# Attention weights split into fp16 hi and lo in the first stage, kept in DRAM, and loaded as fp16

## The chip, the cores and the metric

The kernel runs on one core of a Trainium2 chip. The metric is the device time of one execution in microseconds (us), and the median of several runs is what versions are compared by. The engines of the core, by the names of the profile: PE is TensorE (matmuls; PEld is its weight loads), DVE is VectorE, ACT is ScalarE, POOL is GpSimd, SP is SyncE, which only issues DMA transfers here. PEq, SPq and so on are the instruction queues of these engines.

## The reference

A decoder trunk of two layers on a sequence of 512 tokens, width 1024. Layer A is a gated short convolution, layer B is sparse attention over a key/value side that is computed once after layer A; each is followed by a squared-ReLU MLP. All inputs and the output are float32.

```python
# layer 0 (A)
h = rms_norm(x, norm_mix[0])
b, c, u = split(h @ a_w_in, 3)                  # 1024 -> 3 x 1024
x = x + (b * conv3(c * u)) @ a_w_out
x = x + square(relu(rms_norm(x, norm_mlp[0]) @ mlp_w1[0])) @ mlp_w2[0]   # 1024 -> 4096 -> 1024
# shared key/value side
kv = rms_norm(x, kv_norm) @ w_kv                # 6 parts of 4 groups x 64
k_cmp = silu(blocks(kv[0]) @ phi_k_w1) @ phi_k_w2     # 31 blocks, 2048 -> 256 -> 64
v_cmp = silu(blocks(kv[1]) @ phi_v_w1) @ phi_v_w2
# layer 1 (B)
q, gates = rms_norm(x, norm_mix[1]) @ b_w_qg    # 16 heads x 64, and 48 gates
o = gates[0]*attn(q, k_cmp, v_cmp) + gates[1]*attn(q, k_sel, v_sel) + gates[2]*attn(q, k_win, v_win)
x = x + o @ b_w_o
x = x + square(relu(rms_norm(x, norm_mlp[1]) @ mlp_w1[1])) @ mlp_w2[1]
out = rms_norm(x, final_norm)
```

The three attentions are causal, with a relative-position bias added to the logits. With these sizes every selected block and the whole window lie within the sequence, so that two of them are full causal attentions and one goes over 31 compressed blocks.

## The kernel before

**Products.** Every matmul is fp16, and keeps nearly fp32 precision by a split: a value is scaled and written as hi (fp16) and lo = value - hi (fp16), and a product is hi x hi + hi x lo + lo x hi (`mm3`, lines 338 to 341). Activations are kept transposed, features on the partitions, 512 tokens along the free axis; a weight tile of 128 x 128 is the stationary operand.

**Weights.** They come in pieces, listed in order of use in `pieces`. An ordinary piece is 1024 fp32 columns on 128 partitions (512 KB). It goes through three steps. `load_piece` loads it on SP's queue into a staging tile `wst` (three of them). `convert_piece` makes `whi` on ACT (line 193) and `wlo` on DVE (line 194), four buffers of each. `next_piece` hands it to the matmuls. Conversions run two pieces ahead of use (`ahead`), and a conversion is followed by as many loads as staging tiles are free. Within attention the conversion is made in two halves of 512 columns (`ahead_fine`, `convert_piece(512)`), emitted between matmuls. Weights of the second MLP matrices go another way (`down_blocks`, tiles `wst2`, lines 180 to 183), which combines blocks of them first.

**The first stage** (tile pool `first`, lines 222 to 482). The input is transposed chunk by chunk on PE (`x_chunk`: `x0h` on ACT, `x0l` on DVE, line 288 and 289), while six accumulators collect the first pass of the in-projection. The row scale (`x_rstd`, then `rs_r`, `rb`, `rb2`) is applied as the accumulators are read. Passes 1 to 3 have three products each (`pc`, `pu`, `pb`), each of two pieces and 48 matmuls, with six PSUM banks in rotation; the reader of `pc` is `cv_t` (line 446). Then come the four passes of the out projection, with the residual, its squares and the split for the MLP. The bias table goes through DRAM (`ext_d`). Then the first MLP follows (pool `hidden_a`).

**Attention** (pool `attn`). First keys, values, gates and the queries of group 0 are made one after the other. Then a list of items is worked off: a `Full` item is one head of one block of 128 queries in one of the two full branches, a `Cmp` item one block of a group in the compressed branch. An item has the steps st0 (logits on PE, bias and minimum on DVE as `at_s` and `at_m`, exponential on ACT as `at_p`), st1 (transpose on PE, `at_ph` on ACT), st2 (`at_pl` on DVE), st3 (product with the values) and st4 (transposition of the output for the projection). The steps of several items are interleaved by fixed leads:

```python
lead = {1: 2, 2: 3, 3: 4, 4: 6}
...
credit += 1.7 if i < 64 else 0.9
```

Between items the background generator advances by `credit` steps: raw keys, query group 1, phi of the keys, raw values, phi of the values, query groups 2 and 3, half of the output projection. `queries` writes `Q` on ACT and POOL; `raw` writes `kr_hl` and copies it by DMAs on SP into `big`, which the phi matmuls read. The other half of the output projection follows the last item, and then the second MLP (pool `hidden_b`).

Within each engine the instructions run in the order of its own queue. That order is set when the kernel is built, by a scheduler that takes program order as priority and may move an instruction ahead where its operands are due earlier.

Of the kernel before, what the change touches and what calls it, by code (L numbers as in the profile page):

```python
# [10 lines left out]
F32 = mybir.dt.float32  # L11
# [37 lines left out]
def body(ctx, tc, x, rel_bias, norm_mix, norm_mlp, mlp_w1, mlp_w2, a_w_in, a_conv_w, a_w_out,  # L49
         kv_norm, w_kv, cmp_pe_k, cmp_pe_v, phi_k_w1, phi_k_w2, phi_v_w1, phi_v_w2,  # L50
         b_w_qg, b_w_o, final_norm, ident_c, onehot_c, out):
    nc = tc.nc
# [23 lines left out]
    def cols(w, c0, n, scale, k0=0, kn=8):  # L76
        pieces.append((w[k0 * 128:(k0 + kn) * 128, c0:c0 + n].rearrange("(c p) n -> p c n", p=128),
                       (kn, n), scale))
# [13 lines left out]
    def mlp_pieces(layer):  # L92

        for half in range(2):
            for p in range(8 * half, 8 * half + 8):
                up_pair(mlp_w1[layer], p)
            for p in range(4):
                down_blocks(mlp_w2[layer], p, half)

    def block(w, c0, scale=SW, k0=0, kn=8):  # L100
        for k in range(k0, k0 + kn, 4):
            cols(w, c0, 256, scale, k, 4)
# [12 lines left out]
        block(w_kv, part * 256)  # L115
    cols(b_w_qg[0], 1024, 48, SW)
    block(b_w_qg[0], 0)
    block(w_kv, 0)
    block(b_w_qg[0], 256)
    block(phi_k_w1, 0, SW, 0, 16)  # L120
# [6 lines left out]
    for g in range(0, 4, 2):  # L127
        for p in range(4):
            cols(b_w_o[0], p * 256, 256, SW, 2 * g, 4)
    mlp_pieces(1)  # L130

    NS, NW, AHEAD, PIECE = 3, 4, 2, 1024
# [11 lines left out]
    def blocked(i):  # L144
        return pieces[i][1] is None

    def load_piece():
        i = pos["dma"]
        if i >= len(pieces):
            return  # L150
        src, shape, _ = pieces[i]
        if shape is None:
            t = wk[0].tile([128, PIECE2], F32, name="wst2", bufs=NS2)
            for k, u in enumerate(src):
                nc.sync.dma_start(t[:, k * PIECE:k * PIECE + 512].rearrange("p (j n) -> p j n", j=2), u)
        else:
            t = wpool.tile([128, PIECE], F32, name="wst", bufs=NS)
            a, n = shape
            v = t[:, :a * n].rearrange("p (a n) -> p a n", a=a)
            if len(src.shape) == 4:  # L160
                v = v.rearrange("p a (j n) -> p a j n", j=2)
                for j in range(2):
                    nc.sync.dma_start(v[:, :, j], src[:, :, j])
            else:
                nc.sync.dma_start(v, src)
        staged[i] = t
        pos["dma"] += 1

    def convert_piece(step=1024):

        i = pos["cv"]
        if i >= len(pieces):
            return
        _, shape, sc = pieces[i]
        t = staged.pop(i)
        pos["cv"] += 1
        if shape is None:
            b = t.rearrange("p (k b n) -> p k b n", k=2, n=128)
            for e, o, x, y in W_SUMS:
                DVE.tensor_tensor(b[:, :, o], b[:, :, x], b[:, :, y], op=e)  # L180
            hi, lo = (wk[0].tile([128, 2, 7, 128], F16, name=n, bufs=NW2) for n in ("whi2", "wlo2"))
            ACT.activation(hi, b[:, :, 1:], AF.Copy, scale=sc)  # L182
            DVE.scalar_tensor_tensor(lo, b[:, :, 1:], sc, hi, op0=OP.mult, op1=OP.subtract)  # L183
            ready[i] = (hi, lo)
            yield
        else:
            a, n = shape
            hi = wpool.tile([128, PIECE], F16, name="whi", bufs=NW)
            lo = wpool.tile([128, PIECE], F16, name="wlo", bufs=NW)
            for s in range(0, a * n, step):  # L190
                e = min(s + step, a * n)
                w = t[:, s:e]
                ACT.activation(hi[:, s:e], w, AF.Copy, scale=sc)  # L193
                DVE.scalar_tensor_tensor(lo[:, s:e], w, sc, hi[:, s:e], op0=OP.mult, op1=OP.subtract)  # L194
                yield
            r = lambda w: w[:, :a * n].rearrange("p (a n) -> p a n", a=a)
            ready[i] = (r(hi), r(lo))
        while pos["dma"] < len(pieces):
            like = [j for j in range(pos["cv"], pos["dma"]) if blocked(j) == blocked(pos["dma"])]
            if len(like) >= (NS2 if blocked(pos["dma"]) else NS):  # L200
                break
            load_piece()

    def next_piece():

# [11 lines left out]
    def drain(gen):  # L217
        for _ in gen:
            pass
# [169 lines left out]
    for p in range(4):  # L389
        pc, pu, pb = [], [], []  # L390
        if p == 0:
            for dst in (pc, pu, pb):
                dst += [acc(), acc()]

            def first_pairs(dst, w, c):
                part = 1 if dst is pc else 2 if dst is pu else 0
                for m in range(2):
                    mm3(dst[m], [u[:, part, m * 128:(m + 1) * 128] for u in w], [u[:, c] for u in xs],
                        c == 0, c == 7)

            hi = [x_chunk(0), x_chunk(1)]
            for c in range(6):
                w = next_piece()
                if c == 0:
                    load_x(6, 8)
                for dst in (pc, pu, pb):
                    first_pairs(dst, w, c)
                with tc.issue_after(hi[c + 1].ins):
                    drain(ahead())
                hi.append(x_chunk(c + 2))  # L410
            with tc.issue_after(hi[5].ins):
                r0 = x_rstd()
            pr = broadcast_rows(r0)
            rby = row_tile(pr, SY / (SW * SX))
            rb2 = ftile("rb2", 1)
            DVE.tensor_tensor(rb2, rby, rby, op=OP.mult)
            ws = [next_piece(), next_piece()]
        if p == 1:

            ext = wk[0].tile([H, EXT], F32, name="ext")  # L420
            POOL.memset(ext[:, 0:PAD], NEG)
            pe_ = bank("e")
            PE.matmul(pe_[0:H, :], relb, onehot, start=True, stop=True)
            ACT.activation(ext[:, PAD:], pe_[0:H, :], AF.Copy, scale=SL)
            ext_d = dram.tile([H, EXT], F32, name="ext_d")
            nc.scalar.dma_start(ext_d, ext)
            pet = const.tile([128, 2, 16], F32, name="pet")
            pp = bank("e")
            for i in range(2):
                PE.transpose(pp[:, i * 16:(i + 1) * 16], pe_in[:, i], ident[0:16, 0:16])  # L430
            ACT.activation(pet.rearrange("p a b -> p (a b)"), pp[:, 0:32], AF.Copy)
        for dst in (pc, pu, pb):
            if p:
                dst += [acc(), acc()]
                pair(xs, dst)
            else:
                for k in range(2):
                    first_pairs(dst, ws[k], 6 + k)
            drain(ahead())
            for m in range(2):  # L440
                ch = 2 * p + m
                if dst is pc:
                    if m == 0:
                        tmps = []
                    t = ftile("cv_t", 2)
                    DVE.scalar_tensor_tensor(t, pc[m], 1.0 / (SY * SY), rb2, op0=OP.mult, op1=OP.mult)
                    tmps.append(t)
                elif dst is pu:
                    if m == 0:
                        convs = []  # L450
                    v = ftile("cv_v", 2, S + 2)
                    DVE.memset(v[:, 0:2], 0.0)
                    DVE.tensor_tensor(v[:, 2:], pu[m], tmps[m], op=OP.mult)
                    cw = [vec[:, 40 + 8 * k + ch:41 + 8 * k + ch] for k in range(3)]
                    o = ftile("cv_o", 2)
                    ACT.activation(o, v[:, 0:S], AF.Copy, scale=cw[0])
                    for k in (1, 2):
                        DVE.scalar_tensor_tensor(o, v[:, k:k + S], cw[k], o, op0=OP.mult, op1=OP.add)
                    convs.append(o)
                else:  # L460
                    b = ftile("cv_b", 2)
                    DVE.tensor_tensor(b, pb[m], rby, op=OP.mult)
                    DVE.tensor_tensor(b, b, convs[m], op=OP.mult)
                    split_to(ys[0][:, ch], ys[1][:, ch], b)
# [6 lines left out]
    for p in range(4):  # L471
        po = [acc(), acc()]
        pair(ys, po)
        if p < 3:
            drain(ahead())
        for m in range(2):
            residual_in(po[m], 2 * p + m, 1.0 / (SY * SW))
            ss.add(X[:, 2 * p + m])
        for m in range(2):
            split_gain(xs, 2 * p + m, X[:, 2 * p + m], "mlp0")  # L480
        drain(ahead())
    first.__exit__(None, None, None)


# [754 lines left out]
```

## Time and profile before

| what | value |
|---|---|
| median of 3 runs | 1150.83 us (1150.39 to 1152.06) |
| the profiled execution | 1151.28 us, its span 1149.5 us |
| mean granted TensorE clock | 0.994 |
| DMA moved | 115.76 MB, mean 101 GB/s |

The span is from the first to the last instruction. Line numbers (L193) are those of the kernel before. "out<-in" are the tiles that an instruction writes and reads; a row of waits reads "who waited <- for whom: us in total, times, longest". Successive matmuls overlap in the records, so that a busy PE is not one at its peak.

### The profile page before, as it was taken

The numbers are of one execution on the slowest core, as the hardware profiler recorded it, in microseconds if no ns is written. First come the engines' busy times: TensorE is split into PE (matmuls) and PEld (weight loads), VectorE is DVE, ScalarE is ACT, GpSimd is POOL, SyncE is SP. The second block draws the span as 40 slices with busy tenths as digits, with TensorE's granted clock in tenths as the row PEclk, the third lists the DMA queues.
The fourth block names the chain that finished last, engine by engine and source line by source line (L and its number), as shares of the span: only waits on it lengthen the run. The fifth ranks groups of instructions, "written<-read, shape, count | busy, mean of one in ns | idle before, by whom it ended". The sixth has DMA issues, their size and how long they took to land.

```text
span 1149.5 us, 20386 instructions
## 1 busy us (share of the span) xinstructions
PE 1106.0 (96%) x7959; PEld 694.1 (60%) x7959; DVE 837.8 (73%) x1604; ACT 582.7 (51%) x983; POOL 162.2 (14%) x211
## 2 busy tenths in 40 slices
PE   9999999999999999999999899999999999999996
PEld 4444444447884458868466665765444688445885
DVE  4755557765897557988487898997985588754795
ACT  4523235345333444457679778676644534343452
POOL 0000000422000220000120023111132200022031
PEclk9999999999999999999999999999999999999998
DMA  6433235433433333314333530111643343330231
GB/s 208 130 92 110 92 111 174 119 93 93 127 98 108 109 110 107 97 55 122 110 79 99 143 94 19 57 38 38 186 126 99 88 126 110 104 99 19 75 92 74
DMA packets 149379, 115.76 MB, mean 101 GB/s; under 512 B 8612, under 2 KB 146564, under 8 KB 149284
## 3 DMA queue, kind: packets, MB, share of 16 engines
q1 hardware_dynamic: 146736, 109.47, 31.8%
q10 hardware_dynamic: 2260, 4.40, 1.3%
q8 instruction: 62, 1.02, 0.4%
q0 software_dynamic: 288, 0.61, 0.2%
q14 instruction: 33, 0.27, 0.1%
HBM read 110.22 MB, written 2.14 MB: 98 GB/s over the span
## 4 chain that ended last, share of the span: by engine, by line
PE 49%; DVE 20%; ACT 12%; issue 8%; POOL 6%; DMA 4%; SPq 0%; DVEq 0%; ACTq 0%; POOLq 0%
POOL ml_z L501 6%; PE a L340 4%; PE a L339 4%; PE a L341 4%; DVE wlo L183 4%; DMA wst<-mlp_w_dram 4%; ACT rh L502 3%; PE b L339 3%; PE b L340 3%; PE b L341 3%; PE c L341 3%; PE c L339 3%; PE c L340 3%; DVE wst L180 3%; DVE wlo L194 3%
## 5 line engine op out<-in xcount | busy, mean ns | idle before, releaser
L193 ACT ACTIVATE whi<-wst 128x1024 f16<-128x1024 f32 (+2 forms) x171 | 142.2, 857 | 128.3 <-PE b L340 40.0
L194 DVE SCALAR_TENSOR_TENSOR wlo<-wst,whi 128x1024 f16<-128x1024 f32 (+2 forms) x171 | 168.1, 990 | 47.3 <-ACT whi L193 47.1
L501 POOL TENSOR_TENSOR ml_z<-ml_z 128x256 f32<-128x256 f32 x128 | 101.1, 811 | 604.5 <-ACT ml_z L499 403.9
L182 ACT ACTIVATE whi<-wst 128x1792 f16<-128x1792 f32 x64 | 107.0, 1692 | 132.6 <-DVE wst L180 107.8
L341 PEld LDWEIGHTS <-wlo 128*128 128x128 f16 x1024 | 100.1, 98 | 109.3 <-DVE wlo L194 0.7
L339 PEld LDWEIGHTS <-whi 128*128 128x128 f16 x1024 | 100.4, 98 | 108.1 <-issue 3.7
L503 DVE TENSOR_TENSOR rl<-ml_z,rh 128x1792 f16<-128x1792 f32 x32 | 64.8, 2025 | 136.9 <-ACT rh L502 136.9
L340 PEld LDWEIGHTS <-whi 128*128 128x128 f16 x1024 | 100.2, 98 | 105.0 <-issue 1.7
L183 DVE SCALAR_TENSOR_TENSOR wlo<-wst,whi 128x1792 f16<-128x1792 f32 x64 | 129.8, 2033 | 3.6 <-ACT whi L182 3.6
L180 DVE TENSOR_TENSOR wst<-wst 128x256 f32<-128x256 f32 x256 | 105.9, 455 | 24.1 <-DMA wst<-mlp_w_dram 23.1
L502 ACT ACTIVATE rh<-ml_z 128x1792 f16<-128x1792 f32 x32 | 54.3, 1697 | 103.4 <-POOL ml_z L501 103.4
L550 PEld LDWEIGHTS <-wlo 128*128 128x128 f16 x896 | 88.1, 98 | 16.6 <-issue 5.1
L549 PEld LDWEIGHTS <-whi 128*128 128x128 f16 x896 | 88.1, 98 | 14.8 <-issue 3.9
L548 PEld LDWEIGHTS <-whi 128*128 128x128 f16 x896 | 88.2, 98 | 11.0
L499 ACT ACTIVATE ml_z<-ml_t 128x1024 f32<-128x1024 f32 x32 | 33.8, 1057 | 90.5 <-DVE ml_t L497 90.5
L341 PE MATMUL b<-xsh,wlo 128*128 128x512 f16 x208 | 78.8, 379 | 0.0
L340 PE MATMUL b<-xsl,whi 128*128 128x512 f16 x208 | 78.8, 379 | 0.0
L339 PE MATMUL b<-xsh,whi 128*128 128x512 f16 x208 | 78.7, 379 | 0.0
L922 ACT ACTIVATE at_p<-at_s,at_m 128x128 f32<-128x128 f32 (+3 forms) x128 | 71.3, 557 | 13.4 <-DVE at_m L919 13.0
L549 PE MATMUL a<-rl,whi 128*128 128x256 f16 x256 | 70.3, 275 | 4.6 <-DVE rl L503 4.6
L339 PE MATMUL c<-xsh,whi 128*128 128x512 f16 x192 | 72.8, 379 | 0.0
L340 PE MATMUL c<-xsl,whi 128*128 128x512 f16 x192 | 72.8, 379 | 0.0
(312 smaller groups left out, 2757.5 us busy)
## 6 DMA issues: line engine op xcount, KB each, us to landing
wst<-mlp_w_dram SPq DMA_DIRECT2D x256, 256.0 KB, 3.4
wst<-a_w_in_dram SPq DMA_DIRECT2D x18, 512.0 KB, 3.6
wst<-w_kv_dram SPq DMA_DIRECT2D x12, 512.0 KB, 3.7
T<-ext_d ACTq DMA_DIRECT2D x4, 1056.0 KB, 6.0
wst<-a_w_out_dram SPq DMA_DIRECT2D x8, 512.0 KB, 3.5
wst<-b_w_qg_dram SPq DMA_DIRECT2D x8, 512.0 KB, 4.3
wst<-b_w_o_dram SPq DMA_DIRECT2D x8, 512.0 KB, 3.5
wst<-a_w_in_dram SPq DMA_DIRECT2D x8, 384.0 KB, 5.5
```

The source lines that it names most:

```text
L180: DVE.tensor_tensor(b[:, :, o], b[:, :, x], b[:, :, y], op=e)
L182: ACT.activation(hi, b[:, :, 1:], AF.Copy, scale=sc)
L183: DVE.scalar_tensor_tensor(lo, b[:, :, 1:], sc, hi, op0=OP.mult, op1=OP.subtract)
L193: ACT.activation(hi[:, s:e], w, AF.Copy, scale=sc)
L194: DVE.scalar_tensor_tensor(lo[:, s:e], w, sc, hi[:, s:e], op0=OP.mult, op1=OP.subtract)
L339: PE.matmul(ps, w[0], xs[0], start=start, stop=False)
L340: PE.matmul(ps, w[0], xs[1], start=False, stop=False)
L341: PE.matmul(ps, w[1], xs[0], start=False, stop=stop)
L501: POOL.tensor_tensor(z[:, o], z[:, a], z[:, b], op=e)
L502: ACT.activation(rh[0][:, p], z[:, 1:8], AF.Copy)
L548: PE.matmul(acc7[i], wh, xh, start=c == 0 and not other, stop=False, skip_group_check=other)
L549: PE.matmul(acc7[i], wh, xl, start=False, stop=False, skip_group_check=other)
```

## The change

The 26 full pieces that are used from the raw keys on (`w_kv` parts 0 and 1, `b_w_qg` groups 1 to 3, the first weights of both phi, `b_w_o`) are listed in `early`. In the first stage `keep_load` loads them as fp32 on SP into `kp_w` (two tiles), and `keep` makes `kp_h` on ACT and `kp_l` on DVE (two tiles each) and stores both in DRAM on POOL's queue. `keep(2)` stands behind each of the nine products of passes 1 to 3 and in the four passes of the out projection. In attention such a piece is loaded as fp16 straight into `whi` and `wlo` by two DMAs on SP, as soon as it is less than three pieces ahead of the next use, and its conversion is only a hand-over. The other pieces go the old way.

```diff
@@ the list of pieces
     block(b_w_qg[0], 0)
+    early = [len(pieces)]
     block(w_kv, 0)
...
+    early = [i for i in range(early[0], len(pieces)) if pieces[i][1][0] * pieces[i][1][1] == 1024]
+    kept = {}
     mlp_pieces(1)
@@ load_piece
-        if shape is None:
+        if i in early:
+            t = []
+            for name, d in zip(("whi", "wlo"), kept[i]):
+                w = wpool.tile([128, PIECE], F16, name=name, bufs=NW)
+                nc.sync.dma_start(w, d)
+                t.append(w.rearrange("p (a n) -> p a n", a=shape[0]))
+        elif shape is None:
@@ convert_piece
-        if shape is None:
+        if i in early:
+            ready[i] = tuple(t)
+        elif shape is None:
...
+        load_pieces()
+
+    def load_pieces():
         while pos["dma"] < len(pieces):
-            like = [j for j in range(pos["cv"], pos["dma"]) if blocked(j) == blocked(pos["dma"])]
-            if len(like) >= (NS2 if blocked(pos["dma"]) else NS):
+            i = pos["dma"]
+            if i in early:
+                full = i >= pos["use"] + NW - 1
+            else:
+                like = [j for j in range(pos["cv"], i) if j not in early and blocked(j) == blocked(i)]
+                full = len(like) >= (NS2 if blocked(i) else NS)
+            if full:
                 break
             load_piece()
+
+    keeping = {}
+
+    def keep_load(n):
+        for i in early[len(keeping):len(keeping) + n]:
+            src, (a, m), _ = pieces[i]
+            keeping[i] = wk[0].tile([128, PIECE], F32, name="kp_w", bufs=2)
+            nc.sync.dma_start(keeping[i].rearrange("p (a n) -> p a n", a=a), src)
+
+    def keep(n):
+        for i in early[len(kept):len(kept) + n]:
+            t, sc = keeping[i], pieces[i][2]
+            hi, lo = (wk[0].tile([128, PIECE], F16, name=m, bufs=2) for m in ("kp_h", "kp_l"))
+            ACT.activation(hi, t, AF.Copy, scale=sc)
+            DVE.scalar_tensor_tensor(lo, t, sc, hi, op0=OP.mult, op1=OP.subtract)
+            kept[i] = [dram.tile([128, PIECE], F16, name=f"kept{i}{m}") for m in "hl"]
+            for d, w in zip(kept[i], (hi, lo)):
+                nc.gpsimd.dma_start(d, w)
+            keep_load(1)
@@ in passes of the in-projection, behind each product
             drain(ahead())
+            if p == 0 and dst is pb:
+                keep_load(2)
+            if p:
+                keep(2)
@@ in passes of the out projection
         drain(ahead())
+        keep(2)
+    assert len(kept) == len(early)
```

## The prediction

> **What bounds the kernel now.** I read the page first, for the busy times and their course over the span.
>
> ```profile
> span 1149.5 us, 20386 instructions
> PE 1106.0 (96%) x7959; PEld 694.1 (60%) x7959; DVE 837.8 (73%) x1604; ACT 582.7 (51%) x983; POOL 162.2 (14%) x211
> PE   9999999999999999999999899999999999999996
> DVE  4755557765897557988487898997985588754795
> ```
>
> The reader is to see that TensorE (PE) is in its highest digit almost everywhere, and that VectorE (DVE) is half idle in slices 3 to 6 and seven to nine tenths busy in slices 21 to 29. PE's busy time flatters it, since successive matmuls overlap in the records, so the next view was the busy time by stages: conv mixer (45 to 137 us), its out projection (137 to 179), attention (540 to 820), and within attention the conversions alone (DVE's line L194, then ScalarE's, ACT's, line L193).
>
> ```profile
> core 0: us, PE busy (x) PEld busy (x) DVE busy (x) ACT busy (x) POOL busy (x), PEclk, DMA share, GB/s
> 45.00:137.00 92.00, 92.00 (x426) 41.22 (x425) 52.60 (x71) 28.11 (x34) 0.00 (x0) 1.00 0.34 104
> 137.00:179.00 42.00, 42.00 (x196) 19.06 (x195) 24.45 (x31) 16.71 (x22) 0.00 (x0) 1.00 0.33 101
> 540.00:820.00 280.00, 260.93 (x2638) 170.83 (x2637) 231.31 (x717) 208.20 (x565) 45.13 (x59) 1.00 0.28 80
> ...
> sum 280.00, DVE 44.21; mean DVE 3.68
> ...
> sum 280.00, ACT 38.14; mean ACT 3.18
> ```
>
> In the first two rows PE never pauses, while DVE is busy 57% and ACT 30 to 40% of the time: work added there on DVE and ACT has room. In attention PE is idle for at least 280 - 260.9 = 19.1 us, DVE is busy 83% and ACT 74%, and the conversions are 44.2 of DVE's 231.3 us. The third view is who makes PE wait there, matmuls and weight loads (PEld) taken apart.
>
> ```profile
> PE c L928 <- DVE at_pl L934: 5.4, 7, 1.5
> PE b L914 <- DVE at_m L919: 3.2, 6, 1.5
> PE c L886 <- POOL o L963: 2.3, 2, 2.0
> PE b L914 <- POOL Q L739: 1.9, 3, 0.9
> PE d L946 <- ACT at_ph L931: 1.4, 5, 0.6
> ...
> PEld c L928 <- DVE at_pl L934: 9.9, 22, 1.6
> PEld L946 <- ACT at_ph L931: 5.9, 14, 0.8
> PEld L914 <- POOL Q L739: 3.9, 4, 1.4
> PEld c L886 <- POOL o L963: 3.4, 4, 2.5
> PEld c L928 <- ACT at_p L922: 2.2, 4, 1.5
> ```
>
> Many short waits, not one long one: the softmax chain of an item goes PE, DVE, ACT, PE, ACT, DVE, PE, and each engine takes its queue in order, so a conversion of 0.7 us that stands ahead of an `at_pl` or `at_ph` delays the next transpose or product. Those on DVE and ACT add up to 5.4 + 9.9 + 3.2 + 1.4 + 5.9 + 2.2 = 28.0 us, those on GpSimd (POOL) to 11.5 us. So attention is bound by PE's work plus some 19 to 40 us of hand-overs, and the first stage by PE alone.
>
> **Removed from attention.** 26 pieces of 1024 columns (w_kv and phi first weights, queries 1 to 3, the output projection) lose their split. They were split in halves:
>
> ```profile
> L194 DVE SCALAR_TENSOR_TENSOR wlo<-wst,whi 128x512 f16<-128x512 f32 x54 | 37.8, 713 | 7.3 <-ACT whi L193 7.3
> L193 ACT ACTIVATE whi<-wst 128x512 f16<-128x512 f32 x54 | 32.3, 624 | 14.5 <-PE a L340 6.0 <-issue 4.0 <-PE a L700 2.5
> ```
>
> 52 halves are 52 x 0.713 = 37.1 us of DVE and 52 x 0.624 = 32.4 us of ACT. None of it is PE's own work, so the most that can come back is the 28.0 us of waits on these two engines, and the least is nothing, if the waits are plain latency of the chain. Between these ends I go by how full the queues are. DVE's busy to idle time is 231.3 to 48.7, a ratio of 4.7; without the 37.1 us, in a stage 15 us shorter, it is 194.2 to 70.8, or 2.7, 42% less. ACT's goes from 2.9 (208.2 to 71.8) to 2.0, 32% less. Waits that shrank alike would give 28.0 x 0.42 = 12 us. I take **15 us**, because the conversions are among the longest instructions of the queue and come in runs of two to four, so they cause more than their share; this is an estimate. The waits on POOL stay.
>
> **Added in the first stage: the split.** The same 26 pieces are converted there at 1024 columns; near rows of this size and form are
>
> ```profile
> 33.64 1.05 ACT L193 ACTIVATE whi<-wst 128x1024 f16<-128x1024 f32 x1
> 34.72 1.22 DVE L194 SCALAR_TENSOR_TENSOR wlo<-wst,whi 128x1024 f16<-128x1024 f32 x1 [0.43 <-ACT whi L193]
> ...
> ACT whi L193 <- PE c L340: 28.8, 7, 4.1
> ```
>
> 26 x 1.22 = 31.7 us of DVE and 26 x 1.05 = 27.3 us of ACT, over about 150 us. From 45 to 179 us DVE would go from 77 to about 106 of 134 us and ACT from 45 to 67. The cover is PE's unbroken work and the lead of the conversions: ACT waits for PE to free a weight buffer (28.8 us in 7 waits on one line alone), so conversions run ahead of need, and a `kp` instruction ahead of one is absorbed. If that cover failed at the four pass ends, a yl or a residual two instructions late would cost about 2.4 us each; I put **1 us** (0 to 5).
>
> **The start is where there is no cover.** In the order of the built instructions the first six splits stand before about 45 us: four `kp_h` ahead of the last x0h on ACT, two more ahead of `rb`, and two `kp_l` on DVE between the steps of the first rstd. The chain there before the change:
>
> ```profile
> 26.57 0.69 ACT L288 ACTIVATE x0h<-e,vec 128x512 f16<-128x512 f32 x1 [2.90 <-PE e L372]
> 36.00 0.30 ACT L296 ACTIVATE rs_r<-ss,eps 128x4 f32<-128x4 f32 x1
> 37.15 0.67 ACT L288 ACTIVATE x0h<-e,vec 128x512 f16<-128x512 f32 x1
> 39.86 0.16 DVE L303 SCALAR_TENSOR_TENSOR rs_r<-rs_t,rs_r 128x4 f32<-128x4 f32 x1
> 40.83 0.60 ACT L315 ACTIVATE rb<-e 128x512 f32<-128x512 f32 x1 [3.02 <-PE e L310]
> 42.26 0.69 DVE L446 SCALAR_TENSOR_TENSOR cv_t<-a,rb 128x512 f32<-128x512 f32 x1
> 46.22 0.39 PE L339 MATMUL a<-x0h,whi 128*128 128x512 f16 x1
> 46.44 0.38 PE L340 MATMUL a<-x0l,whi 128*128 128x512 f16 x1
> ```
>
> The idle 2.9 us before each x0h hides most of the four `kp_h` (4.2 us): the last x0h comes 1 to 2 us late. ACT's square root (rs_r) now stands behind that x0h, at about 40.5 instead of 36.0, and then two `kp_l` of 1.22 us and a reordered wlo lie in the DVE part, so rs_r of DVE is ready at about 45.8, 6 us late, and the first `cv_t` ends at about 49 instead of 42.95. It frees the bank in which pass 1 of the convolution begins, at 46.22 now: 3.3 us of slack eat half of it. **3 us** lost (1 to 7).
>
> **Added: transfers.** 26 fp32 loads on SP's queue, 52 fp16 stores from POOL, and 52 fp16 loads on SP in attention, in place of 26 fp32 loads of the same bytes.
>
> ```profile
> wst<-a_w_in_dram SPq DMA_DIRECT2D x18, 512.0 KB, 3.6
> rb<-final_norm_dram POOLq DMA_DIRECT2D x2, 256.0 KB, 3.7
> big<-kr_hl SPq DMA_DIRECT2D x8, 128.0 KB, 2.4
> ...
> 5.00:15.00 10.00, 9.32 (x44) 4.79 (x44) 5.97 (x9) 5.03 (x9) 0.00 (x0) 1.00 1.04 334
> ```
>
> From 45 to 179 us the DMA engines are a third busy with one load of 512 KB for each piece that PE uses. The change adds as much again in loads and as much again in stores: 3 x 0.34 = 1.02 by bytes, 312 GB/s where the busiest ten microseconds show 334 at a share of 1.04. That is full, but the weights are loaded three pieces ahead, some 15 us, and land after 3.6 us, so they can be several microseconds late at no cost. A POOL transfer of 256 KB lands after 3.7 us, and a split buffer is due again after two pieces, 10 us. I take 0 here (0 to 20, the ends in the rivals). The Trainium skill, "DMA: Bandwidth & Descriptors", section "Issuing engines are not separate DMA queues", speaks against the change at this place: transfers issued from SP, ACT and POOL interleave on the same 16 engines. No run yet shows POOL's stores beside SP's loads; by that rule the 1.02 holds in full, without it the loads alone make 0.68.
>
> In attention SP's loads wait for PE to free one of four buffers, where they waited for the conversion; they are issued three pieces ahead, at least 2 x 24 matmuls at a start every 0.22 us (the last two rows of the start), over 10 us, for a load of about 4. Behind them on SP stand the `kr_hl` copies (2.4 us) that the phi matmuls need; the second half of the copies now waits for the first half of the next query product. The phi matmuls come only after that product's second half, so I count nothing (up to 10 us, below).
>
> **The sum.** The profiled execution took 1151.28 us, its span 1149.5, and 0.45 us lies between it and the median of 1150.83. 1151.3 - 15 + 3 + 1 = 1140.3; **1140 us**.
>
> **Rivals.**
> *The waits are latency.* PE's items are emitted with fixed leads of two to six, and if the chain's own length sets the waits, freeing DVE and ACT returns 3 us or less: 1151.3 - 3 + 4 = 1152. For it: PE waits on DVE also in stretches with few conversions. Against: DVE at 83%, with waits mostly on the two engines that are relieved. 14%.
> *The first stage starves (slower).* The transfers' share passes 1 from 45 to 179 us, wst lands late, and PE stops between pieces. At a need of 1.02 the 134 us would stretch by 3 us; at 1.15, if mixed reads and writes are less efficient, by 20 us, of which perhaps 2 are covered: 1151.3 - 15 + 4 + 18 = 1158. It decides once the stage loses over 11 us, a share of 1.08. For it: the 1.02. Against: a DMA packet of a larger row costs less per byte, and the loads made ahead of need. 12%. The rule of the Trainium skill above ("DMA: Bandwidth & Descriptors", same section) speaks for this rival.
> *A new wait in attention.* The copies behind SP's waiting loads make phi late by one piece (5.2 us), twice: 1140 + 10 = 1150. 5%.
> *All waits on DVE and ACT go.* 1151.3 - 28 + 4 = 1127. It needs every item to run at PE's pace. 11%.
> That the split does not move is excluded by the built order: 26 `kp_h` stand in the first stage and no conversion of these pieces in attention.
>
> **Chances.** The forecast (gain of 8 to 22 us in attention, loss of 1 to 8) has 58%, 1131 to 1148. A measurement of this kernel tells about 0.2%, 2.3 us, from no change. Faster by more: 0.58 + 0.11 + a quarter of 0.14 + part of the new wait = 0.74; within: 0.08; slower: 0.12 + the rest of the latency case = 0.18. The range takes in the latency and the new-wait cases, all but the far ends of the other two: 1126 to 1156.
>
> **What would show it.** Right: in the stage that now ends at 820 us, PE idle shorter by some 15 us with DVE's busy time down by 37; waits on at_pl and at_ph roughly halved; waits on POOL as they are. The first matmul of pass 1 at about 49 us, and no pause of PE from there to 179. DMA share in that stretch at 0.8 to 1.0. Wrong: PE pauses between 50 and 179 us released by wlo or a wst load; waits in attention unchanged with DVE at 73% or less; or PE waiting for a whi or wlo that a load, not DVE, releases.

## The result, and the profile after

The changed kernel took 1166.9 us (median of 5 runs, 1163.44 to 1167.84) where the kernel before took 1150.83 (5 runs, 1150.39 to 1152.68): a ratio of 1.0131 (of the means), with an interval of 1.0113 to 1.015. It is slower by 1.3%; 1140 us was forecast, in a range of 1126 to 1156. The profiled execution has a span of 1165.1 us, 15.6 more than the 1149.5 before.

The head of the page of the changed kernel:

```profile
PE 1110.3 (95%) x7959; PEld 694.9 (60%) x7959; DVE 836.7 (72%) x1580; ACT 583.2 (50%) x959; POOL 185.3 (16%) x263
...
PE   9799889999999999999999899999999999999996
...
DMA  7979873633333333313433441010552343330221
```

PE had its highest digit in all slices but one and the last; now there are three more below 9, in slices 2, 5 and 6, all in the first stage, where the DMA digits are 7 to 9. DVE and ACT have the same busy time as before (837.8 and 582.7): the work has been moved, not saved.

Busy time by stages, changed kernel (columns as in the prediction: us of the stretch, then busy time and instructions of PE, PEld, DVE, ACT and POOL, PE's granted clock, DMA share, GB/s). The first two rows are the conv mixer from its pass 1 on and its out projection; the third is the stretch of attention with the 2638 matmuls that filled 540 to 820 us before.

```profile
54.00:159.00 105.00, 95.28 (x437) 42.10 (x437) 70.24 (x87) 44.42 (x51) 21.58 (x40) 1.00 0.85 281
159.00:204.00 45.00, 43.09 (x192) 19.03 (x190) 30.39 (x40) 18.88 (x26) 0.00 (x0) 0.96 0.43 132
...
562.00:836.00 274.00, 258.85 (x2638) 171.04 (x2636) 202.95 (x668) 183.96 (x515) 44.20 (x59) 1.00 0.28 83
```

Attention gave back 280 - 274 = 6 us for the same matmuls. The first stage lost nearly four times that. Before, 426 matmuls filled 92 us without a pause; at that pace the 437 of the first row need 94.4 us and took 105 (10.6 lost), and the 192 of the second, at the pace of 196 in 42, need 41.1 and took 45 (3.9 lost). The rest was lost before pass 1, as the timeline shows (start, duration, engine, line, operation; in brackets the idle time before it and what ended that):

```profile
25.67 1.06 ACT L237 ACTIVATE kp_h<-kp_w 128x1024 f16<-128x1024 f32 x1 [4.09 <-DMA kp_w<-w_kv_dram]
...
32.43 1.06 ACT L237 ACTIVATE kp_h<-kp_w 128x1024 f16<-128x1024 f32 x1 [3.45 <-DMA kp_w<-b_w_qg_dram]
...
43.89 0.67 ACT L328 ACTIVATE x0h<-e,vec 128x512 f16<-128x512 f32 x1
...
50.71 0.15 DVE L343 SCALAR_TENSOR_TENSOR rs_r<-rs_t,rs_r 128x4 f32<-128x4 f32 x1
...
54.48 0.38 PE L379 MATMUL a<-x0h,whi 128*128 128x512 f16 x1
```

The first matmul of pass 1 starts at 54.48 instead of 46.22, 8.3 us late. So 8.3 + 10.6 + 3.9 = 22.8 lost, 6 gained, which makes 16.8 where the span grew by 15.6; about 1 us came back elsewhere, between the first MLP and attention.

The waits in the first stage (0 to 206 us) of the changed kernel, in us, count and longest:

```profile
ACT kp_h L237 <- DMA kp_w<-b_w_o_dram: 21.1, 8, 6.6
...
ACT kp_h L237 <- DMA kp_w<-b_w_qg_dram: 16.0, 6, 3.5
ACT whi L205 <- PE b L380: 12.8, 5, 4.1
...
ACT kp_h L237 <- DMA kp_w<-w_kv_dram: 9.5, 3, 4.4
ACT kp_h L237 <- DMA kp_w<-phi_v_w_dram: 8.7, 4, 2.9
...
ACT kp_h L237 <- DMA kp_w<-phi_k_w_dram: 2.8, 1, 2.8
```

ACT stands 21.1 + 16.0 + 9.5 + 8.7 + 2.8 = 58.1 us at a `kp_h` whose `kp_w` has not landed. Before, in the same stretch, ACT's waits were of another kind, its largest being

```profile
ACT whi L193 <- PE b L340: 35.0, 12, 4.1
```

a `whi` that waits for PE to free a buffer, so ACT was ahead; of that row 12.8 us are left. One place of the kind in the changed kernel's timeline, and the last `whi` before it that waited for PE:

```profile
72.88 1.06 ACT L205 ACTIVATE whi<-wst 128x1024 f16<-128x1024 f32 x1 [3.91 <-PE c L380]
...
137.39 1.06 ACT L237 ACTIVATE kp_h<-kp_w 128x1024 f16<-128x1024 f32 x1 [6.64 <-DMA kp_w<-b_w_o_dram]
138.36 1.04 ACT L205 ACTIVATE whi<-wst 128x1024 f16<-128x1024 f32 x1
...
139.43 1.23 DVE L206 SCALAR_TENSOR_TENSOR wlo<-wst,whi 128x1024 f16<-128x1024 f32 x1 [3.50 <-ACT whi L205]
...
139.45 0.39 PE L379 MATMUL b<-x0h,whi 128*128 128x512 f16 x1 [2.09 <-ACT whi L205]
```

ACT idles 6.64 us for a piece that nothing needs before attention, some 400 us later. Behind it in ACT's queue stands the `whi` that PE needs now; it follows without a gap, then `wlo`, and PE has paused for it.

Not this one wait alone did that. At 72.88 us the conversions still had their full lead: the `whi` waited for PE to free the oldest of four buffers, three pieces, or some 3 x 5.2 = 15.6 us, ahead of its use (PE works 24 x 92 / 426 = 5.2 us on a piece). The next nine `whi`, up to the one at 138.36, start 7.3 us apart on average, and so the lead is gone at 139 us. Between the two rows ACT ran 14 `kp_h`: 14.8 us of work, and 36.6 us of waits for `kp_w`. The weights themselves were there: from 40 to 206 us a single `whi` waited for its own `wst`, for 1.8 us.

The waits of PE in attention, 562 to 836 us:

```profile
PEld c L974 <- DVE at_pl L980: 6.3, 17, 1.4
...
PEld L992 <- ACT at_ph L977: 3.9, 11, 0.7
...
PEld L960 <- POOL Q L785: 3.6, 4, 1.3
PEld c L932 <- POOL o L1009: 3.6, 3, 2.1
...
PE c L974 <- DVE at_pl L980: 3.2, 4, 1.0
PE b L960 <- DVE at_m L965: 3.0, 5, 1.5
PEld c L974 <- ACT at_p L968: 2.5, 6, 1.2
...
PE c L932 <- POOL o L1009: 2.1, 2, 1.6
...
PE b L960 <- POOL Q L785: 1.8, 3, 0.8
...
PE d L992 <- ACT at_ph L977: 0.5, 1, 0.5
```

Those on DVE and ACT are 6.3 + 3.9 + 3.2 + 3.0 + 2.5 + 0.5 = 19.4 us instead of 28.0; those on POOL 11.1 instead of 11.5.

### The profile page after: what moved, and what is told of

The parts are those of the page before. It is cut to its first block, busy times and chain, and to the rows that moved or that the text cites. A ratio compares the mean times of both kernels' runs of the same rounds, so it can differ in the third digit from the quotient of the medians.

```text
span 1165.1 us, 20546 instructions
## 1 busy us (share of the span) xinstructions
PE 1110.3 (95%) x7959; PEld 694.9 (60%) x7959; DVE 836.7 (72%) x1580; ACT 583.2 (50%) x959; POOL 185.3 (16%) x263
## 4 chain that ended last, share of the span: by engine, by line
PE 43%; DVE 20%; ACT 11%; DMA 9%; issue 8%; POOL 7%; SPq 1%; DVEq 0%; ACTq 0%; POOLq 0%
POOL ml_z L547 6%; ACT rh L548 3%; PE a L379 3%; PE a L381 3%; PE a L380 3%; DVE wlo L206 3%; DVE ml_t L543 2%; PE b L379 2%; PE b L380 2%; PE b L381 2%; DVE wlo L195 2%; ACT ml_z L545 2%; DMA wst<-mlp_w_dram 2%; DMA kp_w<-b_w_o_dram 2%; DMA kp_w<-b_w_qg_dram 2%
## 5 line engine op out<-in xcount | busy, mean ns | idle before, releaser
L206 DVE SCALAR_TENSOR_TENSOR wlo<-wst,whi 128x1024 f16<-128x1024 f32 (+4 forms) x121 | 131.9, 1096 | 23.8 <-ACT whi L205 23.6
L205 ACT ACTIVATE whi<-wst 128x1024 f16<-128x1024 f32 (+4 forms) x121 | 110.8, 943 | 53.3 <-PE b L380 20.3
L965 DVE CUSTOM_DVE_ANT_0 at_s<-b,T 128x128 f32<-128x128 f32 (+3 forms) x128 | 60.9, 481 | 26.9 <-PE b L961 15.2
```

## The experiments

Three theories were held at first, in the words of this text. **Order**: a `kp_h` that waits for its load blocks ACT's queue. **Transfers**: the traffic itself is too much, and weights land late. **Engines**: 59 us more work on DVE and ACT is too much for the stage. All kernels are edits of the changed kernel; four of them are shown by their difference from another experiment, which the text names. A ratio is of means, to the kernel before, run on the same chip, with its 95% interval. Expected times compare with the ratio times 1150.83.

**The two halves of the change.** Attention alone: one piece is split and stored in the first stage, and all 26 places in attention load that pair (other weights, the same work).

```diff
         for i in early[len(kept):len(kept) + n]:
+            if kept:
+                kept[i] = kept[early[0]]
+                continue
...
-            keep_load(1)
...
-                keep_load(2)
+                keep_load(1)
```

> Only the first of the 26 pieces is split and stored in the first stage; all 26 loads in attention read that one pair (its values stand in for the other 25 pieces', so the output is not the reference's). This is the attention half of the change without the first-stage half. If the two halves add: 1150.8 minus the 7 us that attention came back in the changed kernel, 1143 to 1145, and the first stage as before (the out projection's first matmul at 140 us). If the 15 us that were forecast are there and the first stage's lateness hid them: 1134 to 1138.

The first stage alone: everything is split and stored, but attention loads and converts as before.

```diff
-        if i in early:
+        if False:
...
-        if i in early:
+        if False:
...
-            if i in early:
-                full = i >= pos["use"] + NW - 1
-            else:
-                like = [j for j in range(pos["cv"], i) if j not in early and blocked(j) == blocked(i)]
-                full = len(like) >= (NS2 if blocked(i) else NS)
+            like = [j for j in range(pos["cv"], i) if blocked(j) == blocked(i)]
+            full = len(like) >= (NS2 if blocked(i) else NS)
```

> All 26 pieces are split and stored in the first stage, but attention loads fp32 and converts as in the kernel before; the stored copies are not read. If the halves add: 1150.8 + 22.8 = 1172 to 1175. If attention's own order had lost something that the removed conversions only partly gave back, the sum of both halves differs from the changed kernel by more than 3 us.

Attention alone: 0.9953 (0.9939 to 0.9967), a gain of 5.4 us. The first stage alone: 1.0159 (1.0121 to 1.0197), 1169 us where 1172 to 1175 was expected. The halves add to +1.12% where the change has +1.31%, within the intervals, so no interplay shows. Busy time by stages, attention alone:

```profile
538.00:812.00 274.00, 258.81 (x2642) 171.41 (x2640) 202.76 (x668) 183.88 (x514) 44.23 (x59) 1.00 0.27 83
```

This is the row of the changed kernel again: 274 us, PE idle for 15 of them. What attention returns is 5 to 6 us, whatever happens in the first stage.

**Half of the transfers.** Without stores (one pair is stored, the rest is split and dropped), and without loads (all splits read the first two `kp_w` tiles). Both leave the work of ACT and DVE as it is. Without stores the order of their instructions in the first stage is that of the changed kernel, too; without loads the build places several splits elsewhere, so that this kernel is the less clean test.

```diff
+            if not kept:
...
+            else:
+                kept[i] = kept[early[0]]
```

> Loads and splits of all 26 pieces stay; only the first pair is stored, and attention reads that pair 26 times (its values stand in for the others). Takes a third of the first stage's transfers away: by bytes the share falls from 0.9 to about 0.65. If the transfers' throughput is the cause, kp_w lands after 4 us instead of 5.5 to 6 and most of the 14.8 us lost between pass 1 and the MLP go: 1152 to 1156. If two kp_w tiles and the issue-to-landing time of one load are the cause, a load is still asked for only when the split before the last is done: ACT's waits on kp_w fall by a third and 1160 to 1164 is left. If it is the inserted DVE and ACT work itself: 1165 to 1167.

```diff
+            if len(keeping) >= 2:
+                keeping[i] = keeping[early[len(keeping) % 2]]
+                continue
```

> Only two pieces are loaded into kp_w; all 26 splits read these two tiles and all stores stay (24 pieces get other pieces' values). No split waits for a transfer in but the first two. If throughput or the wait for kp_w is the cause, both vanish: 1145 to 1155, what is left being the start. If the inserted work on ACT and DVE is the cause, the loss stays: 1163 to 1167.

No stores: 0.9977 (0.9961 to 0.9992). No loads: 1.001 (0.9991 to 1.0028). Attention's part being -0.47%, the first stage now costs 0.24% and 0.57%, where it cost 1.78% with both: most of its loss goes either way. Without stores the time comes to 1148 us, below all three expectations, the lowest of which was 1152 to 1156. No stores, by stages and by DMA issues (KB each, us to landing):

```profile
110.00:140.00 30.00, 30.00 (x141) 13.62 (x140) 25.36 (x32) 16.76 (x19) 0.00 (x0) 1.00 0.65 208
```

```profile
wst<-a_w_in_dram SPq DMA_DIRECT2D x18, 512.0 KB, 4.5
...
kp_w<-b_w_o_dram SPq DMA_DIRECT2D x8, 512.0 KB, 4.0
```

PE is unbroken in the middle of the passes, with all the splits on ACT and DVE: the engines' work is not the cause, and that theory falls. What is left without stores lies at the start, where pass 1 begins at 50.53 us (46.22 before, 54.48 in the changed kernel). The same two loads in the changed kernel:

```profile
wst<-a_w_in_dram SPq DMA_DIRECT2D x18, 512.0 KB, 5.3
...
kp_w<-b_w_o_dram SPq DMA_DIRECT2D x8, 512.0 KB, 6.0
```

POOL's stores make SP's loads land up to 2 us later (3.6 us for `a_w_in` before the change). That fits what the Trainium skill says in "DMA: Bandwidth & Descriptors", "Issuing engines are not separate DMA queues": transfers of different issuers interleave on the same engines, and these runs agree. Up to here both order and transfers fit: fewer transfers also shorten the wait at `kp_h`.

**Holding the splits at the start only.** The build may put no `kp_h` ahead of the bias table's `ext`, and no `kp_l` ahead of `rb2`; then the same with four `kp_w` tiles instead of two, so that loads are issued earlier.

```diff
-            ACT.activation(hi, t, AF.Copy, scale=sc)
-            DVE.scalar_tensor_tensor(lo, t, sc, hi, op0=OP.mult, op1=OP.subtract)
+            with tc.issue_after(held[1].ins):
+                ACT.activation(hi, t, AF.Copy, scale=sc)
+            with tc.issue_after(held[0].ins):
+                DVE.scalar_tensor_tensor(lo, t, sc, hi, op0=OP.mult, op1=OP.subtract)
...
-            DVE.tensor_tensor(rb2, rby, rby, op=OP.mult)
+            held.append(DVE.tensor_tensor(rb2, rby, rby, op=OP.mult))
...
-            ACT.activation(ext[:, PAD:], pe_[0:H, :], AF.Copy, scale=SL)
+            held.append(ACT.activation(ext[:, PAD:], pe_[0:H, :], AF.Copy, scale=SL))
```

> The changed kernel, with every split held on ACT behind the bias table's copy of pass 1 (ext) and on DVE behind rb2: none stands in the chain of the first rstd. The work and the transfers are the same. The start should be as before the change (pass 1 at 46 to 48 us instead of 54). If the transfers' throughput is the main cause, the same 27 MB have less time and the loss between pass 1 and the MLP stays at 12 to 18 us: 1156 to 1163 (ratio 1.005 to 1.010). If the loss came from the order at the start alone: 1146 to 1148.

```diff
-            keeping[i] = wk[0].tile([128, PIECE], F32, name="kp_w", bufs=2)
+            keeping[i] = wk[0].tile([128, PIECE], F32, name="kp_w", bufs=4)
...
-                keep_load(2)
+                keep_load(4)
```

> As with the hold, and four kp_w tiles instead of two, four loads asked for at the outset. If what holds ACT is the time from the issue to the landing of a load that is asked for too late, four tiles ask 10 us earlier, ACT's waits on kp_w (58 us in the changed kernel) fall below 15 and the time comes to 1146 to 1150. If the transfers' throughput is the limit, deeper tiles move nothing: within 3 us of the kernel with the hold alone.

Held: 1.0144 (1.0114 to 1.0174). Held with four tiles: 1.0116 (1.0089 to 1.0142). Neither is a cure. The first, 1167 us, lies above both of its expectations; the second, by its ratio, is 3 us better, about what was expected if the transfers were the limit. Held start, by stages:

```profile
30.00:50.00 20.00, 18.50 (x89) 8.27 (x87) 15.53 (x26) 14.17 (x21) 1.13 (x2) 1.00 0.47 146
80.00:110.00 30.00, 30.00 (x141) 13.58 (x140) 17.23 (x19) 12.22 (x13) 7.04 (x13) 1.00 0.98 336
110.00:140.00 30.00, 24.76 (x113) 10.51 (x111) 20.79 (x27) 12.97 (x15) 7.04 (x13) 1.00 0.92 303
140.00:170.00 30.00, 19.47 (x69) 7.40 (x70) 20.39 (x23) 12.95 (x15) 5.42 (x10) 0.78 0.75 255
```

The start is good (pass 1 begins at 45.70 us), PE is even unbroken from 80 to 110 us at a DMA share of 0.98, and the whole loss appears later: 113 matmuls instead of 141 from 110 to 140 us, and 69 from 140 to 170, in the last pass and the out projection, which starts at 149 us. With four tiles ACT's waits change their cause:

```profile
ACT kp_h L239 <- DVE kp_l L241: 11.5, 7, 2.5
...
ACT kp_h L239 <- DMA kept122h<-kp_h: 6.2, 1, 6.2
```

The load has come, but now `kp_h` waits for its output buffers (two `kp_h`, two `kp_l`, freed by DVE and by the stores). It stands ahead of a due `whi` as before. By itself this pair would fit late transfers as well.

**Each split behind the conversions that are due.** A `kp_h` may not stand ahead of the last `whi` that was emitted before it, a `kp_l` not ahead of the last `wlo`, and a load of `kp_w` not ahead of the last `wst` load. Instructions and bytes are the same as in the change.

```diff
-                nc.sync.dma_start(v, src)
+                last["s"] = nc.sync.dma_start(v, src)
...
+                last["a"] = ACT.activation(hi[:, s:e], w, AF.Copy, scale=sc)
+                last["d"] = DVE.scalar_tensor_tensor(lo[:, s:e], w, sc, hi[:, s:e], op0=OP.mult, op1=OP.subtract)
...
+            with tc.issue_after(last["s"].ins):
+                nc.sync.dma_start(keeping[i].rearrange("p (a n) -> p a n", a=a), src)
...
+            with tc.issue_after(last["a"].ins):
+                ACT.activation(hi, t, AF.Copy, scale=sc)
+            with tc.issue_after(last["d"].ins):
+                DVE.scalar_tensor_tensor(lo, t, sc, hi, op0=OP.mult, op1=OP.subtract)
```

> The changed kernel, with each split held behind the last weight conversion that program order has ahead of it on ACT and DVE, and each load of kp_w behind the last weight load on SP: same work, same bytes, but a split can no longer stand ahead of a conversion that is due sooner. If transfers' throughput is the cause: 1155 to 1162, since the need is still one split piece for each weight piece. If the cause is the order, a split waiting for its load ahead of a due conversion: 1145 to 1149 (start and stage as before, attention 5 to 8 us shorter).

0.9952 (0.9933 to 0.997), 1147.02 us: the whole loss of the first stage is gone. By stages and by ACT's waits (40 to 206 us):

```profile
45.00:137.00 92.00, 92.00 (x426) 41.36 (x426) 71.93 (x89) 45.22 (x52) 19.34 (x36) 1.00 0.88 293
137.00:179.00 42.00, 42.00 (x197) 19.01 (x195) 33.75 (x40) 23.80 (x30) 8.83 (x17) 1.00 0.94 305
```

```profile
ACT whi L206 <- PE b L384: 28.8, 11, 4.1
...
ACT kp_h L240 <- DMA kp_w<-b_w_qg_dram: 4.4, 5, 2.2
...
ACT kp_h L240 <- DMA kp_w<-w_kv_dram: 1.5, 2, 1.0
...
ACT kp_h L240 <- DMA kp_w<-b_w_o_dram: 0.4, 1, 0.4
```

PE is as unbroken from 45 to 179 us as before the change, while the DMA engines are busier (0.88 and 0.94) than in the slower kernel (0.85 and, later, 0.43). So the transfers are not the cause by themselves. ACT again waits for PE, and at `kp_h` only 6.3 us.

**Which of the holds it is.** Of the paced kernel's holds, first ACT's and DVE's alone, then SP's alone (both edits are to the paced kernel).

```diff
-            with tc.issue_after(last["s"].ins):
-                nc.sync.dma_start(keeping[i].rearrange("p (a n) -> p a n", a=a), src)
+            nc.sync.dma_start(keeping[i].rearrange("p (a n) -> p a n", a=a), src)
```

> Half of the pacing: splits held behind the due conversions on ACT and DVE, the loads of kp_w left where the build puts them on SP. If what cost the time is a split that stands in ACT's queue ahead of a due conversion and waits there for its load: as with the full pacing, 1145 to 1150 (ratio 0.994 to 0.998). If it is loads of kp_w ahead of weight loads in SP's queue: 1160 or more.

```diff
-            with tc.issue_after(last["a"].ins):
-                ACT.activation(hi, t, AF.Copy, scale=sc)
-            with tc.issue_after(last["d"].ins):
-                DVE.scalar_tensor_tensor(lo, t, sc, hi, op0=OP.mult, op1=OP.subtract)
+            ACT.activation(hi, t, AF.Copy, scale=sc)
+            DVE.scalar_tensor_tensor(lo, t, sc, hi, op0=OP.mult, op1=OP.subtract)
```

> The other half: loads of kp_w held behind weight loads on SP, the splits free on ACT and DVE. The build still puts two splits in a row ahead of a due conversion. If the order on ACT is the cause: a loss of 10 us or more between pass 1 and the MLP, ratio 1.005 to 1.015. If the order on SP is: 0.994 to 0.998.

ACT and DVE held: 0.9946 (0.9924 to 0.9968), 1146.85 us. Loads held: 1.0086 (1.0055 to 1.0117). ACT and DVE held, by stages and by DMA issues:

```profile
137.00:179.00 42.00, 42.00 (x196) 19.07 (x195) 33.63 (x40) 23.98 (x30) 8.66 (x17) 1.00 0.93 295
```

```profile
kp_w<-b_w_o_dram SPq DMA_DIRECT2D x8, 512.0 KB, 6.8
```

Loads held, by stages and by ACT's waits:

```profile
137.00:179.00 42.00, 35.65 (x155) 15.38 (x154) 28.11 (x33) 18.56 (x22) 8.67 (x16) 0.92 0.84 282
```

```profile
ACT kp_h L239 <- DMA kp_w<-b_w_o_dram: 21.4, 6, 7.0
```

With the engines held the `kp_w` loads land even later (6.8 us against 6.0) and nothing is lost; with the loads held `kp_h` waits longer than in the change (74.0 us against 49.0, from 40 to 206 us), and PE stops. The cause is the place of `kp_h` in ACT's queue (and of `kp_l` in DVE's; the two were not parted). Late loads alone do no harm; it takes both, since without the stores, in the same bad order, the loads came early enough for it to cost nothing after the start.

**Fewer pieces.** The paced kernel with only the first 13 of the 26 pieces, one split at each place instead of two.

```diff
+    early = early[:13]
...
-                keep(2)
+                keep(1)
```

> Only the first 13 of the 26 pieces are kept, one behind each product, paced as in the run before; the other 13 are converted in attention. The transfers' share of the first stage falls to about 0.68 and both theories expect no loss there. Attention keeps the part of its gain that lies in the first half of the pieces, where conversions stand densest: 3 to 5 of about 7 us. 1146 to 1149, a ratio of 0.995 to 0.998.

0.9997 (0.9981 to 1.0014): no gain, where half of it would be 0.9976. The first stage is not where it went: attention takes 232.8 us from the first `at_s` to the last `at_pl`, where it took 233.4 before and 229.7 in the paced kernel. The gain is not in proportion to the pieces; which of them carry it is open.

The version that holds ACT and DVE beats both kernels: 0.9946 to the kernel before, and by that 0.9946 / 1.0131 = 0.982 to the changed one. From the paced kernel (0.9952) it can't be told apart.

## Why the prediction was wrong

**"A `kp` instruction ahead of one is absorbed"** (1 us, 0 to 5) is the step that failed, together with the 0 for transfers. Each was right in what it counted. The splits' 59 us on DVE and ACT cost PE nothing after the start in the kernel without stores, and nothing at all in the first stage of the paced one; and the share came out at 0.85 in the changed kernel's passes and at 0.88 to 0.94 in the paced kernel, as "0.8 to 1.0" said. What was left out stood between the two terms: the change adds a wait, `kp_h` for its load, and the step did not ask what is queued behind the waiting instruction. The price of a `kp_h` was taken as its 1.05 us; it was 1.05 plus up to 6.64 us of waiting. The waits for PE on which the step relied, 4.1 us at the longest, are what ACT had to spare at most for each piece of 5.2 us. With the waits at `kp_h` a `whi` came every 7.3 us, and from 72.88 to 139 us the lead of some 16 us, three pieces, ran out. Cost: 10.6 + 3.9 = 14.5 us instead of 1.

**The start**, 3 us (1 to 7), was 8.3. The mechanism was right: splits ahead of the last x0h, then the square root, then `rs_r`, `rb` and `cv_t`. The size was off for the same reason. The last x0h was put 1 to 2 us late and came at 43.89 instead of 37.15, 6.7 us late, since three `kp_h` ahead of it waited 4.09, 3.45 and 1.58 us for loads that the sum had taken as landed. `rs_r` of DVE, foreseen at 45.8, ended at 50.9.

**Attention**, 15 us (8 to 22), was 6 in the profile and 5.4 in the runs. What the step said of the queues came about. The conversions on DVE (line L206, the same stretch) are down from 44.2 us to

```profile
562.00:836.00 274.00, 8.26 (x11) 1.00 0.28 83
```

by 36 us for the 37 foreseen; all of DVE fell by 28.4 us only. Its other instructions are as many as before (717 - 61 = 656 then, 668 - 11 = 657 now), but records of successive instructions overlap and busy time counts an overlap once, so durations can't be taken off it in full, as the prediction did. DVE's busy to idle time is 202.95 to 71.05, a ratio of 2.9 where 2.7 was expected. The waits on POOL stayed. Two sizes were off. The waits fell by 31% (28.0 to 19.4), not by 42%, and the step from 12 to 15 us had no row behind it. And a us of wait is not a us of time: before, waits on DVE, ACT and POOL were 28.0 + 11.5 = 39.5 us in a stretch where PE was idle for 19.1, now 19.4 + 11.1 = 30.5 against 15.1. So half of what is listed is no idle time of PE: most of it, 25.3 of the 39.5 us, is PEld's, and PE's matmuls can still be running then. The 12 us of the ratio times 19.1 / 39.5 would have been 5.8. That is arithmetic after the event; that the overlap is the reason was not tried; nor was a longer lead of the items, so what keeps the rest of the waits is open.

**The rivals.** "The first stage starves" had the right place and sign, and 1158 us of the 1166.9, with 12%; its mechanism, a share past 1 so that weights land late, is refuted by the paced kernel, which runs from 45 to 179 us at a higher share without a pause. "The waits are latency" was nearer to the truth about attention than the forecast was (3 us or less against 15), though the first stage's 4 us in its sum were wrong as well. "A new wait in attention" was 0.3 us (PE for the `kr_hl` copies), and "all waits go" did not occur.

**What would have told.** The signs named for a wrong prediction did show: pauses of PE between 54 and 179 us released by `whi` and `wlo`. And of what could be read before the run, the order of the built instructions had `kp_h` ahead of `whi` on ACT, as the trace shows it; the price of a wait in that place was missing.

## What to carry to other kernels

Work that is not urgent and waits for a transfer costs, in an in-order queue, the wait as well as its own time to everything urgent behind it: put it behind the work that is due, as here, where the same instructions and bytes went from +1.3% to -0.5%. A share of the DMA engines near 0.9 is no loss in itself; what counts is who stands behind the late load. And before waits are taken as what can be gained, hold their sum against the idle time of the engine that waits.

## What the runs showed of the hardware

A pause of PE can cost more than its length, when the granted clock falls after it. In the kernel with the held start, PE's timeline and, after it, the busy time by fine stretches:

```profile
141.48 0.61 PE L382 MATMUL c<-x0h,whi 128*128 128x512 f16 x1 [3.90 <-ACT whi L205]
```

```profile
143.00:146.00 3.00, 3.00 (x8) 1.07 (x9) 1.21 (x2) 2.00 (x2) 0.54 (x1) 0.50 0.84 271
...
149.00:152.00 3.00, 3.00 (x15) 1.37 (x14) 0.76 (x1) 0.00 (x0) 0.88 (x2) 1.00 1.00 352
```

At a clock of 0.50 a matmul shows 0.6 us instead of 0.39, and PE does 8 in 3 us instead of 15, so the pause of 3.90 us cost some 3 x 7 / 15 = 1.4 us more in that row alone. The Trainium skill, "TensorE: Matmul & The Clock Gate", section "What's actually happening", gives half the clock after an idle window of some 3.4 us and the full one after a busy window as long; this pause agrees. The rule does not cover all that the runs show: in the changed kernel the clock was 0.64 and 0.51 from 36 to 40 us, after two pauses of 1.03 and 0.97 us within 4 us, while one of 1.98 us at 157 us in the kernel with the held start left it at 1.00. None of this was in the prediction, which priced a pause at its length.
